# A two-block model on one core: in the second block, pairs of 64-row products alternate, low-rank columns are regrouped, inversion products are cut into 64-column halves, and the attention output is split late

## The chip, the core and the metric

The kernel runs on one core of one Trainium2 chip. The metric is the device time of one execution in microseconds (us), taken as the median of several runs.

## What is computed

Two layers are applied to a sequence of 1024 tokens of width 1024, all in float32. The change touches the mixer of the second layer alone. Cut to that part, the reference is:

```python
h = rms_norm(x, norm_mix_g)
u = h @ w_in                                  # 1024 x 4736
u_rwkv = centred_token_shift(u[:, :RWKV_COLS], mu_prev, mu_next)
q, k_att, v_att, gl_rwkv, gl_attn = split(u[:, RWKV_COLS:])
# rwkv7_bidir: r, k, v, g_lo and four low-rank inputs wf_lo, wb_lo, af_lo, ab_lo of 64 columns
decay  = exp(-DECAY_SCALE * sigmoid(w0 + tanh(w_lo) @ w_up))      # per direction
a      = sigmoid(a0 + a_lo @ a_up)                                # per direction
# per direction, 8 heads of 64, one step per token:
S = S * w_t - (S @ kk_t) (a_t * kk_t)^T + v_t k_t^T ;  y_t = S @ r_t
# banded_gqa_attention: 8 query heads, 2 key heads, window of 128 to both sides, blocks of 128
merged = sigmoid(gl_rwkv) * (y_rwkv @ w_proj_rwkv) + sigmoid(gl_attn) * (y_attn @ w_proj_attn)
x = x + merged @ w_out
```

The low-rank inputs lie in the columns of `w_in` in the order forward decay, backward decay, forward rate, backward rate, 64 columns each. After the mixer comes a mixture of 16 experts and a final norm.

## The kernel before

The function `phase_c` holds the mixer of the second layer. Features lie on the 128 partitions and tokens along the free dimension; one tile of 128 features holds two heads of 64. The recurrence over tokens is turned into chunks of 64 tokens.

`proj` multiplies the normed input with 37 tiles of 128 columns of `w_in`. Each of these jobs is two halves of 512 tokens, and each half is 24 products in a rounded float32 form (`mm3`, lines 332 to 334). `proj_split` prepares the weights of a job (ScalarE line 327, VectorE line 328). Tiles 13 and 14 are the low-rank inputs: 13 holds the decay columns of both directions, 14 the rate columns. Tiles 15 to 20 feed attention, 21 to 36 are gates. `choose` appends jobs to the list two ahead of the one that runs: the three tiles r, k, v of the next pair of heads once the pair before has its low-rank outputs, and else the next of the others.

`prep(p)` runs four times in a row, once for each pair of heads p, and waits first for its tiles r, k, v. It transposes v (line 1474), sums squares over each head with the product against `hones` (line 1482: a 128-column stationary operand and a moving operand of two columns), and makes the low-rank outputs (line 1508, four products of 64 rows and 512 tokens for each direction d: both halves of the decay, then both of the rate). VectorE then forms the operands AR and BK (lines 1517 to 1543). The products of line 1561 follow in bursts of four, one burst for each head h, each with 64 rows, 128 stationary and 128 moving columns. VectorE masks the result out of PSUM (lines 1564 and 1565), and after two bursts four transposes follow (line 1569, out of PSUM by ScalarE line 1570). There are 64 such bursts. At the end of a prep comes another product against `hones` (line 1610).

`invert(p)` inverts a 32 by 32 triangular matrix per chunk in 31 steps on VectorE (lines 1632, 1633) and completes it with two groups of 16 products (lines 1655, 1673: 128 rows, 128 stationary columns of which each half serves one direction, 32 moving columns). `chain` steps through the 16 chunks in both directions; each step loads its operands by DMA and multiplies in bursts whose 64-column halves alternate. `attn_scores` makes one product of 64 rows for each of 8 heads and 8 blocks (line 1723, up to 384 moving columns), each put out by VectorE (line 1725). `attn_values` multiplies with the values; for each block it then scales (line 1796) and splits the result into a rounded part and a remainder (ScalarE line 1804, GpSimd line 1805). `post_rwkv`, `merge_rwkv` and `merge_attn` finish the mixer.

The order of the instructions on each engine is fixed at build time. All these functions are generators; `weave` resumes the first one in the list whose condition holds in the times that a planner (`Model`) has worked out. A `yield` of a number asks to be resumed so many nanoseconds later, `K.room(tag)` when a PSUM bank is free by the plan, `K.when(...)` when operands are there. In the list, `inverts` and `preps` stand ahead of `chain`, and `proj` stands behind these, so the projection fills what the others leave. PSUM has four banks under the tag `mm` and four under `sm`. SBUF blocks of one size come from a ring.

```python
def room(self, tag):
    return lambda: self.clock.room(tag)
```

## Time and profile before

| | |
|---|---|
| median of 3 runs | 3086.57 us (3083.51 to 3089.09) |
| time of the profiled execution | 3083.45 us |
| its span | 3081.7 us |
| TensorE busy | 2856.3 us (93%) |
| VectorE busy | 2122.4 us (69%) |
| ScalarE busy | 1357.7 us (44%) |
| GpSimd busy | 434.1 us (14%) |
| mean granted TensorE clock | 0.953 |

The span is the time from the first to the last instruction of the profiled execution. In the views of the trace, PE is TensorE's matmul, PEld its weight load, DVE VectorE, ACT ScalarE, POOL GpSimd and SP SyncE, which issues most DMAs. A float32 product appears as two PE records; a product in the rounded form as one. A record's duration is a latency: consecutive records overlap, so a group's cost is read from start to start, or from the group's busy time, which counts overlaps once. PEclk is the share of the full TensorE clock that was granted: 1.00 is 2.4 GHz and 0.50 is 1.2 GHz.

### The profile page before, as it was taken

How to read it: one execution, taken by the hardware profiler on the slowest of the kernel's cores; microseconds unless marked ns; L12 is line 12 of the kernel's file. 1: busy time of each engine (PE TensorE's matmuls, PEld its weight loads, DVE VectorE, ACT ScalarE, POOL GpSimd, SP SyncE). 2: the span in 40 equal slices, each digit the busy share in tenths (PEclk: the TensorE clock that was granted, in tenths of full speed). 3: DMA queues.
4: the chain of work that ended last, by engine and by line, in shares of the span. 5: the costliest groups of instructions: out<-in, count | busy, mean ns of one | idle time of the engine just before them, and what ended most of it. 6: DMA issues, size and time to landing. Idle time of an engine off the chain costs nothing. (4 is left out here: it accounts for less than half of the span.)

```text
span 3081.7 us, 41330 instructions
## 1 busy us (share of the span) xinstructions
PE 2856.3 (93%) x15743; PEld 2300.4 (75%) x15743; DVE 2122.4 (69%) x3039; ACT 1357.7 (44%) x2152; POOL 434.1 (14%) x506
## 2 busy tenths in 40 slices
PE   7989989999999999889999998998799769999995
PEld 3878778788888888677777776776477658888884
DVE  5574655666656666745768675678755989999995
ACT  5442344432122222343343442454522258888885
POOL 2410001000000000322111011034101301211112
PEclk8989999999999999999989988999899989999998
DMA  7421122311111111414444545385143679999994
GB/s 276 151 69 42 55 72 86 116 48 41 42 62 48 48 48 39 127 55 121 112 110 117 123 109 134 110 262 155 52 146 125 247 282 384 395 392 396 396 377 135
DMA packets 381693, 470.42 MB, mean 153 GB/s; under 512 B 151184, under 2 KB 282679, under 8 KB 381495
## 3 DMA queue, kind: packets, MB, share of 16 engines
q1 hardware_dynamic: 374519, 450.97, 43.8%
q0 software_dynamic: 6976, 16.81, 2.3%
q8 instruction: 124, 2.03, 0.3%
q14 instruction: 74, 0.61, 0.1%
HBM read 390.12 MB, written 77.59 MB: 152 GB/s over the span
## 5 line engine op out<-in xcount | busy, mean ns | idle before, releaser
L328 DVE TENSOR_TENSOR wl<-wr,wh 128x1024 fp32r<-128x1024 f32 x534 | 639.7, 1229 | 234.4 <-ACT wh L327 214.8
L327 ACT ACTIVATE wh<-wr 128x1024 fp32r<-128x1024 f32 x536 | 554.1, 1061 | 94.5 <-PE mm L334 52.9
L332 PE MATMUL mm<-h,wh 128*128 128x512 f32 x1296 | 525.6, 406 | 0.0
L334 PE MATMUL mm<-h,wl 128*128 128x512 f32 x1296 | 512.1, 395 | 12.7 <-DVE wl L328 12.7
L333 PE MATMUL mm<-h,wh 128*128 128x512 f32 x1296 | 511.9, 395 | 0.0
L334 PEld LDWEIGHTS mm<-h,wl 128*128 128x128 f32 x1296 | 247.6, 191 | 67.1 <-DVE wl L328 14.0
L332 PEld LDWEIGHTS mm<-h,wh 128*128 128x128 f32 x1296 | 247.9, 191 | 63.2 <-issue 8.3
L333 PEld LDWEIGHTS mm<-h,wh 128*128 128x128 f32 x1296 | 248.1, 191 | 47.5 <-DVE h L535 0.2
L1176 DVE SCALAR_TENSOR_TENSOR u<-pad,par,u 128x1024 f32<-128x1024 f32 x176 | 225.7, 1282 | 6.8 <-ACT u L1173 3.4
L332 PE MATMUL mm<-wh,eh 128*128 128x512 f32 x512 | 201.1, 393 | 0.0
L333 PE MATMUL mm<-wl,eh 128*128 128x512 f32 x512 | 199.7, 390 | 0.0
L334 PE MATMUL mm<-wh,el 128*128 128x512 f32 x512 | 199.6, 390 | 0.0
L1250 DVE TENSOR_TENSOR yacc<-yacc,mm 128x512 f32<-128x512 f32 x144 | 98.9, 686 | 74.8 <-PE mm L334 74.0
L333 PE MATMUL mm<-wl,ah 128*128 128x512 f32 x352 | 137.7, 391 | 1.1 <-DVE wl L328 1.1
L332 PE MATMUL mm<-wh,ah 128*128 128x512 f32 x352 | 138.1, 392 | 0.6 <-ACT wh L327 0.6
L334 PE MATMUL mm<-wh,al 128*128 128x512 f32 x352 | 137.4, 390 | 0.0
L2405 POOL DMA_INDIRECT xacc<-ys,slot x32 | 72.1, 2253 | 440.5 <-ACT ys L2404 435.9
L1162 ACT ACTIVATE pad<-mm 128x512 f32<-128x512 f32 x44 | 26.4, 601 | 238.3 <-PE mm L334 238.3
L332 PE MATMUL mm<-hh,wh 128*128 128x512 f32 (+1 forms) x296 | 119.5, 404 | 0.0
L333 PE MATMUL mm<-hh,wh 128*128 128x512 f32 (+1 forms) x296 | 115.6, 391 | 0.8 <-DVE hh L716 0.8
L334 PE MATMUL mm<-hh,wl 128*128 128x512 f32 (+1 forms) x296 | 115.1, 389 | 0.0
L334 PEld LDWEIGHTS mm<-wh,el 128*128 128x128 f32 x512 | 96.4, 188 | 20.4 <-DVE el L2361 0.2
(468 smaller groups left out, 5693.5 us busy)
## 6 DMA issues: line engine op xcount, KB each, us to landing
wr<-in_exp_w_gate_dram SPq DMA_DIRECT2D x128, 512.0 KB
wr<-in_exp_w_up_dram SPq DMA_DIRECT2D x128, 512.0 KB
wr<-in_exp_w_down_dram SPq DMA_DIRECT2D x128, 512.0 KB
wr<-in_w_in_dram SPq DMA_DIRECT2D x62, 512.0 KB
wr<-in_w_ada_dram SPq DMA_DIRECT2D x48, 512.0 KB
wr<-in_w_up_dram SPq DMA_DIRECT2D x44, 512.0 KB
KB<-KB SPq DMA_DIRECT2D x32, 512.0 KB
wr<-in_w_down_dram SPq DMA_DIRECT2D x22, 512.0 KB
```

What stands on the lines that cost most here:

```text
L327: self.nc.scalar.activation(hi, src, AF.Copy)
L328: (eng or self.nc.vector).tensor_tensor(lo, src, hi.bitcast(F32), SUB)
L332: t.matmul(ps, wh, xh, start=start, stop=False)
L333: t.matmul(ps, wh, xl, start=False, stop=False)
L334: t.matmul(ps, wl, xh, start=False, stop=stop)
L1162: nc.scalar.activation(p[:, 1 + 8 * m:9 + 8 * m, 1:65], ps.rearrange("p (r c) -> p r c", c=64), AF.Copy)
L1176: nc.vector.scalar_tensor_tensor(u, p[:, i // 3:i // 3 + 16, i % 3:i % 3 + 64], w(i), u, op0=MUL, op1=ADD)
L1250: nc.vector.tensor_add(yacc[t][:, s], yacc[t][:, s], ps)
L2405: nc.gpsimd.indirect_dma_start(out=xacc[c], out_offset=bass.IndirectOffsetOnAxis(ap=slot[:, e - 1:e], axis=0), in_=ys[:, s], in_offset=Non ...
```

## The change

The diff below is cut to its core. Six things change, all in the mixer of the second layer.

The products of line 1561 of the two heads, which use rows 0 to 63 and 64 to 127, are issued alternately into two PSUM banks, in 32 bursts of eight in place of 64 bursts of four. The wait between them goes from 900 ns after each to 1800 ns after both.

The low-rank columns are loaded so that tile 13 holds decay and rate of the forward direction and tile 14 those of the backward one. Decay and rate of one direction then use different rows and alternate in pieces of 256 tokens. For this, each of the two weight loads becomes two DMAs, the per-column shift factors are loaded once more in the new order (four small DMAs), and the tanh runs on half the partitions of each of the two tiles.

The scores of two heads alternate in pieces of 128 keys. The products against `hones` and the two products of the inversion are each cut into two halves of 64 stationary columns. The conditions `K.room(tag, 2)` ask for two free banks.

The attention result is kept in float32 blocks, and a new generator `split_att` splits it in two parts on ScalarE and VectorE once the chain is done. The planner's cost for 64-row products is changed to match.

```diff
-            if f(ins[1]) <= 64:
+            if f(ins[1]) <= 64 or ins[0].ap[0][1] == 64:
                 return max(f(ins[0]), f(ins[1])) / 1.2 + 8
-    def room(self, tag):
-        return lambda: self.clock.room(tag)
+    def room(self, tag, n=1):
+        return lambda: max(self.clock.room(tag, 4 - i) for i in range(n))
...
+        for n in ("mu_prev", "mu_next"):
+            lo = a[n + "_2"][0][13 * 128:15 * 128].rearrange("(i d j) -> i d j", i=2, j=64)
+            items.append((n + "_l", [(lo[0], slice(0, 64)), (lo[1], slice(64, 128))], 2))
...
-    job = lambda i: (w_in, 0, 128 * i, 128, 8)
+    job = lambda i: (w_in, 0, (64 * i + 832, 64 * i + 960) if i in (13, 14) else 128 * i, 128, 8)
...
-            if i == 13:
-                nc.scalar.activation(u, u, AF.Tanh)
+            if i in (13, 14):
+                nc.scalar.activation(u[0:64], u[0:64], AF.Tanh)
...
-            nc.tensor.matmul(ps[:, t, :], sq[:, 128 * t:128 * t + 128], hones, start=True, stop=True)
+            for q in hq:
+                nc.tensor.matmul(ps[q, t, :], sq[:, 128 * t + q.start:128 * t + q.stop], hones, start=True, stop=True)
...
-            for i in range(2):
-                for m in range(2):
-                    ps = K.sm()
-                    q = slice(64 * d, 64 * d + 64)
-                    nc.tensor.matmul(ps, Z["up"][q, i, 128 * p:128 * p + 128], R[13 + i][q, off[m]:off[m] + 512], start=True, stop=True)
+            for m in range(2):
+                yield K.room("sm", 2)
+                ps = [K.sm() for _ in range(2)]
+                for n in range(0, 512, 256):
+                    for i in range(2):
+                        q = slice(64 * i, 64 * i + 64)
+                        nc.tensor.matmul(ps[i][:, n:n + 256], Z["up"][q, d, 128 * p:128 * p + 128],
+                                         R[13 + d][q, off[m] + n:off[m] + n + 256], start=True, stop=True)
...
-                    for h in range(2):
-                        q = slice(64 * h, 64 * h + 64)
-                        yield K.room("sm")
-                        ps = K.sm([128, 4, 128])
-                        for i in range(4):
-                            c = 4 * b + i
-                            nc.tensor.matmul(ps[:, i, :], BK[g][q, c].rearrange("p s t -> p (s t)"),
-                                             AR[g][q, c].rearrange("p s t -> p (s t)"), start=True, stop=True)
+                    yield K.room("sm", 2)
+                    pss = [K.sm([128, 4, 128]) for h in range(2)]
+                    for i in range(4):
+                        c = 4 * b + i
+                        for h in range(2):
+                            q = slice(64 * h, 64 * h + 64)
+                            nc.tensor.matmul(pss[h][:, i, :], BK[g][q, c].rearrange("p s t -> p (s t)"),
+                                             AR[g][q, c].rearrange("p s t -> p (s t)"), start=True, stop=True)
...
-                        yield 900
+                    yield 1800
...
-            nc.tensor.matmul(ps[:, c, :], OF[c // 8][:, c % 8, :], Dt[:, c, :], start=True, stop=True)
+            for q in hq:
+                nc.tensor.matmul(ps[q, c, :], OF[c // 8][:, c % 8, q], Dt[:, c, :], start=True, stop=True)
...
-                yield K.room("mm")
-                q = slice(64 * (h % 2), 64 * (h % 2) + 64)
-                ps = K.mm()
-                nc.tensor.matmul(ps[:, :n], q_fm[15 + h // 2][q, 128 * b:128 * b + 128], kd[h // 4][q, 128 * lo:128 * hi], start=True, stop=True)
+                if h % 2 == 0:
+                    yield K.room("mm", 2)
+                    pss = [K.mm() for _ in range(2)]
+                    for i in range(lo, hi):
+                        for x, q in enumerate(hq):
+                            nc.tensor.matmul(pss[x][:, 128 * (i - lo):128 * (i - lo) + 128], q_fm[15 + h // 2][q, 128 * b:128 * b + 128],
+                                             kd[h // 4][q, 128 * i:128 * i + 128], start=True, stop=True)
...
-                nc.scalar.activation(hi_, y[:, 2 * kp:2 * kp + 2, :], AF.Copy)
-                nc.gpsimd.tensor_tensor(lo_, y[:, 2 * kp:2 * kp + 2, :], hi_.bitcast(F32), SUB)
+                nc.vector.tensor_tensor(YQ[b // 4][kp][:, :, tok:tok + 128], po[:, kk, :], y[:, kk, :], MUL)
...
+    def split_att():
+        yield K.after("chain")
+        for m in range(2):
+            yield K.after(("yq", 4 * m + 3))
+            YA[m] = hl_blocks(K, "ya", 2)
+            for kp in range(2):
+                K.split(YQ[m][kp], YA[m][0][kp], YA[m][1][kp])
+                yield False
```

## Rows read from the trace of the kernel before

**Rows 1.** Busy time by stretch: length, PE PEld DVE ACT POOL, PEclk, DMA, GB/s.
```profile
1386.00:1888.00 502.00, 497.07 (x2387) 384.56 (x2385) 342.36 (x592) 198.62 (x289) 66.59 (x58) 0.93 0.46 114
1888.00:1980.00 92.00, 76.02 (x368) 62.67 (x367) 48.85 (x101) 26.74 (x37) 10.02 (x12) 0.87 0.32 87
1980.00:2145.00 165.00, 140.74 (x2744) 113.44 (x2744) 122.59 (x258) 83.71 (x217) 54.86 (x74) 0.95 0.82 238
2145.00:2220.00 75.00, 54.54 (x250) 32.97 (x249) 56.34 (x108) 35.99 (x90) 21.53 (x22) 0.80 0.08 25
1563.55:1587.44 23.89, 23.89 (x72) 17.03 (x72) 9.40 (x14) 14.74 (x23) 0.84 (x1) 0.50 0.55 123
```

**Rows 2.** End of prep 0, start of prep 1, timeline: start us, length.
```profile
1483.84 2.25 PE L1610 MATMUL sm<-hones,ks 128*128 128x2 f32 x15
...
1506.54 1.03 PE L1474 MATMUL sm<-ident,u 128*128 128x128 f32 x8
```

**Rows 3.** After prep 3, timeline of DVE: first inversion step, its wait.
```profile
1914.22 0.20 DVE L1632 TENSOR_TENSOR tmp<-N,M 128x31 f32<-128x31 f32 x1 [23.28 <-POOL M L1627]
```

**Rows 4.** Groups of PE by line: busy us, mean ns, idle before.
```profile
L1561 PE MATMUL sm<-AR,BK 64*128 64x128 f32 x512 | 73.9, 285 | 0.8 <-DVE BK L1543 0.8
L1508 PE MATMUL sm<-u,lora 64*128 64x512 f32 x64 | 40.2, 772 | 0.0
L1673 PE MATMUL sm<-Dt,HT 128*128 128x32 f32 x128 | 24.0, 362 | 0.8 <-ACT HT L1646 0.8
L1655 PE MATMUL sm<-Dt,OF 128*128 128x32 f32 x128 | 17.0, 295 | 0.7 <-ACT Dt L1646 0.7
L1610 PE MATMUL sm<-hones,ks 128*128 128x2 f32 x64 | 8.3, 260 | 3.3 <-DVE ks L1607 3.3
L1482 PE MATMUL sm<-hones,sq 128*128 128x2 f32 x64 | 7.4, 246 | 0.0
L1723 PE MATMUL mm<-katt,qatt 64*128 64x384 f32 (+1 forms) x128 | 36.5, 534 | 0.1
```

**Rows 5.** One burst of line 1561 between projection records, timeline of PE.
```profile
1414.45 0.39 PE L334 MATMUL mm<-h,wl 128*128 128x512 f32 x1
1414.77 1.16 PE L1561 MATMUL sm<-AR,BK 64*128 64x128 f32 x8
1415.85 0.50 PE L332 MATMUL mm<-h,wh 128*128 128x512 f32 x1
```

**Rows 6.** Block 1, alternating 64-row products at PEclk 0.50, timeline of PE.
```profile
169.73 3.79 PE L962 MATMUL sm<-v,kt 64*128 64x128 f32 x32
173.45 0.79 PE L332 MATMUL mm<-hh,wh 128*128 128x512 f32 x1
...
196.17 0.42 PE L979 MATMUL sm<-kq,kq 64*128 64x128 f32 x1
196.18 0.42 PE L980 MATMUL sm<-kq,kq 64*128 64x128 f32 x1
```

**Rows 7.** Chain bursts of alternating 64-column halves, timeline of PE (PEclk 1.00).
```profile
1988.53 1.15 PE L1953 MATMUL sm<-XS,LA 128*64 128x64 f32 x32
1989.51 0.29 PE L1920 MATMUL mm<-LR,XS 128*64 128x64 f32 x4
```

**Rows 8.** Low-rank and inversion products at full, then half clock, timeline of PE.
```profile
1519.99 3.70 PE L1508 MATMUL sm<-u,lora 64*128 64x512 f32 x8
...
1568.49 3.78 PE L1508 MATMUL sm<-u,lora 64*128 64x512 f32 x4
1572.20 7.03 PE L1673 MATMUL sm<-Dt,HT 128*128 128x32 f32 x32
```

**Rows 9.** Waits, 1386 to 1888 us: who, releaser, us, times, longest.
```profile
DVE TA L1564 <- PE sm L1561: 53.2, 32, 3.1
```

**Rows 10.** Attention's split in the kernel before, and VectorE's split of 1024 columns.
```profile
L1805 POOL TENSOR_TENSOR ya<-rd,ya 128x256 fp32r<-128x256 f32 x16 | 11.4, 730 | 62.3 <-ACT ya L1804 62.3
L328 DVE TENSOR_TENSOR wl<-wr,wh 128x1024 fp32r<-128x1024 f32 x31 | 37.8, 1221 | 9.0 <-ACT wh L327 8.8
```

More of the change, by code (lines that the diff above doesn't have):

```diff
@@ L344, in wraw @@
         t = self.blk([128, kt, nc_], name="wr")
+        if isinstance(c0, tuple):
+            n = nc_ // len(c0)
+            for i, c in enumerate(c0):
+                self.nc.sync.dma_start(t[:, :, n * i:n * i + n], w[r0:r0 + kt * 128, c:c + n].rearrange("(k p) c -> p k c", p=128))
+            return t
         self.nc.sync.dma_start(t, w[r0:r0 + kt * 128, c0:c0 + nc_].rearrange("(k p) c -> p k c", p=128))
@@ L1313, in phase_c @@
     nc.vector.tensor_scalar(ka[:, 4:8], ka[:, 0:4], -1.0, 1.0, op0=MUL, op1=ADD)
+    hq = [slice(64 * h, 64 * h + 64) for h in range(2)]
     hones = K.own("hones", [128, 2])
@@ L1503, in prep @@
             th = [K.blk([128, T], name="th") for _ in range(2)]
[L1504 to L1508 removed]
+            for m in range(2):
[6 more added lines that the diff above has]
+                                         R[13 + d][q, off[m] + n:off[m] + n + 256], start=True, stop=True)
+                for i in range(2):
                     dst = rv(th[i])[:, off[m]:off[m] + 512]
[L1510 to L1511 removed]
+                    nc.scalar.activation(dst, ps[i], AF.Tanh, bias=hb[:, 8 * i + 4 * d + p:8 * i + 4 * d + p + 1], scale=0.5)
+                yield True
             tw, ta = th
@@ L1609, in prep @@
         for t in range(8):
-            nc.tensor.matmul(ps[:, t, :], ks[:, 128 * t:128 * t + 128], hones, start=True, stop=True)
+            for q in hq:
+                nc.tensor.matmul(ps[q, t, :], ks[:, 128 * t + q.start:128 * t + q.stop], hones, start=True, stop=True)
         nc.vector.tensor_copy(bonus[:, :, 2 * p:2 * p + 2], ps)
@@ L1654, in invert @@
         for c in range(16):
-            nc.tensor.matmul(ps[:, c, :], OF[c // 8][:, c % 8, :], Dt[:, c, :], start=True, stop=True)
+            for q in hq:
+                nc.tensor.matmul(ps[q, c, :], OF[c // 8][:, c % 8, q], Dt[:, c, :], start=True, stop=True)
         K.mark(("off", p))
@@ L1672, in invert @@
         for c in range(16):
-            nc.tensor.matmul(ps[:, c, :], HT[c // 8][:, c % 8, :], Mt[:, c, :], start=True, stop=True)
+            for q in hq:
+                nc.tensor.matmul(ps[q, c, :], HT[c // 8][:, c % 8, q], Mt[:, c, :], start=True, stop=True)
         yield K.when(ps)
@@ L1703, in phase_c @@
     YA = {}
-    P, ST, Yo, VA = {}, {}, {}, {}
+    P, ST, YQ = {}, {}, {}
     def attn_scores():
@@ L1795, in attn_values @@
             yield K.when(po)
-            nc.vector.tensor_tensor(y, po, y, MUL)
-            ST.pop(b)
-            yield False
             tok = b % 4 * 128
             if tok == 0:
-                YA[b // 4] = hl_blocks(K, "ya", 2)
+                YQ[b // 4] = [K.blk([128, 2, 512], name="yq") for _ in range(2)]
             for kp in range(2):
-                hi_, lo_ = (YA[b // 4][i][kp][:, :, tok:tok + 128] for i in range(2))
-                nc.scalar.activation(hi_, y[:, 2 * kp:2 * kp + 2, :], AF.Copy)
-                nc.gpsimd.tensor_tensor(lo_, y[:, 2 * kp:2 * kp + 2, :], hi_.bitcast(F32), SUB)
-            K.mark(("ya", b))
+                kk = slice(2 * kp, 2 * kp + 2)
+                nc.vector.tensor_tensor(YQ[b // 4][kp][:, :, tok:tok + 128], po[:, kk, :], y[:, kk, :], MUL)
+            ST.pop(b)
+            K.mark(("yq", b))
             yield True
@@ L1809, in attn_values @@
         kd.clear()
+    def split_att():
[6 more added lines that the diff above has]
+                yield False
+            YQ[m].clear()
+            K.mark(("ya", m))
     MG, GT = {}, {}
@@ L1848, in merge_attn @@
         yield K.after("merge_rwkv")
-        yield K.after(("ya", 3))
+        yield K.after(("ya", 0))
         W = [K.wsplit(K.wraw(w_proj[1], 0, 4, 256 * i, 256)) for i in range(4)]
@@ L1856, in merge_attn @@
             if i == 0:
-                yield K.after(("ya", 4 * m + 3))
+                yield K.after(("ya", m))
             if n < 7:
@@ L2110, in phase_c @@
     st.load(2)
-    return MG, x2d, (proj_first(), proj_split(), *before, inverts(), preps(), chain(), values_bonus(), proj(), post_rwkv((3, 2, 1, 0)), attn_values(), post_rwkv((4, 5, 6, 7)), split_y(), attn_scores(), merge_attn(), merge_rwkv())
+    return MG, x2d, (proj_first(), proj_split(), *before, inverts(), preps(), chain(), values_bonus(), proj(), post_rwkv((3, 2, 1, 0)), attn_values(), post_rwkv((4, 5, 6, 7)), split_y(), attn_scores(), split_att(), merge_attn(), merge_rwkv())
 def phase_d(K, MG, x2d, before):
```

19 lines of the change are left out of this document (10 added, 9 removed).

## The prediction, made before the changed kernel was run

> **What bounds the kernel now.** I read first the busy time by stretch over the second mixer, with the borders set at the start of the first prep, the end of the last, the first step of the chain that has all its operands, and the chain's end [rows 1]. Between 1386 and 1888 us PE is busy for 497.1 of 502 us and VectorE for 342.4: the four preps and the projection that fills around them are bound by PE's work. From 1888 to 1980 us PE is busy for 76.0 of 92 us. There the last inversion sets the end: its first step on VectorE waited 23.3 us for a GpSimd memset [rows 3], which stands in GpSimd's queue behind copies that wait for a load. From 1980 to 2145 us the chain goes on at a DMA share of 0.82 with PE at 140.7 of 165 us; it is not bound by PE alone. From 2145 to 2220 us PE is idle a quarter of the time and VectorE is busy for 56.3 of 75 us.
>
> The second look is at whether work saved in a prep can shorten the first stretch. Prep 0 starts its last products at 1483.8 us and prep 1 begins at 1506.5 us [rows 2]: it waits for its own tiles of the projection. In that hole PE runs projection, so a prep that ends earlier finds a longer hole only if PE has no less to do. As PE is never idle, each microsecond of PE work taken out of a prep moves everything behind it, the hole included. That holds as long as projection jobs are left to fill with; PE's 76.0 us after the last prep are mostly such jobs, so the supply doesn't run out before.
>
> The third look is at what the lines of the change cost on PE [rows 4], and the fourth at records that already alternate elsewhere in this kernel [rows 6, 7].
>
> **Products of line 1561.** A burst of four products is eight records. From the projection record before it to the one behind it are 1.40 us [rows 5]; less the 0.21 us that 512 columns take at 2.4 GHz, a burst costs 1.19 us. 64 bursts are 76 us, and the group's busy time says 73.9 [rows 4]. What two heads side by side cost is shown by block 1: two products of 64 rows on the two halves of the rows start 10 ns apart [rows 6]. There 32 records, 16 pairs, fill 3.72 us at half clock, so 0.116 us a pair at full clock, and eight pairs 0.93 us. That is a burst of today without its edges, for two heads. I take half of 73.9: **37 us**. The bounds are 27 (half of the 53.2 us for which VectorE is seen to wait for this line [rows 9]) and 42 (64 bursts of 1.19 become 32 of 1.05).
>
> **Low-rank products.** They are busy for 40.2 us [rows 4] in eight passes. A pass at full clock takes 3.70 us, and half a pass at half clock 3.78 [rows 8]. The changed pass has eight pairs of 256 columns, which is half the time at either clock: 20 us. If the slow passes stay as slow and the edges eat part, 8 x 1.7 = 14; if all run at full clock, 40.2 - 8 x 1.85 = 25. I take **17 us**, nearer to the lower one, since edges stay.
>
> **Products against hones.** 8.3 + 7.4 us in eight groups [rows 4], 1.96 each. The new form has 32 records, 16 pairs of 64-column halves. No row has such halves with two moving columns; the nearest is the chain, where 16 pairs with 64 moving columns take 0.98 us from the start of one burst to the next line [rows 7]. That is 0.98 us less a group, and at most 8 us. The other end is nothing gained. I take **5 us**, near to the chain's row, less two changes of the array's layout.
>
> **Products of the inversion.** 24.0 + 17.0 us in eight groups [rows 4], one of them 7.03 us at half clock [rows 8]. The new form has 64 records, 32 pairs, 1.96 us by the chain's row at full clock. At the clocks of today half is saved, 20; at full clock 41.0 - 8 x 1.96 = 25; if the halves don't overlap well, 10. I take **18 us**; the last two groups lie on the path to the chain itself.
>
> The Trainium skill speaks against these last two: TensorEngine Tiling (Array Packing), Performance Considerations, says that a product with one moving column takes as long as one with 60, and that no tiling should be taken from a dimension that is already small. With 2 and 32 moving columns this is the case here. No row here decides it, since the chain's halves move 64 columns.
>
> **Sum of the first stretch.** 37 + 17 + 5 + 18 = 77 us. All of it is PE work in a stretch that PE bounds.
>
> **Scores of attention.** 36.5 us [rows 4]. The new form has 24 pairs of heads with three blocks of keys and eight with two, that is 88 block pairs or 176 pairs of records; at 0.116 us, 20.4 us, so 16 us of PE are saved. They lie where PE is not the bound [rows 1]. I take a third, **5 us**; the ends are -3 (each pair now waits for two free banks of `mm`, behind which the chain's outputs queue too) and 16.
>
> **The late split.** It takes 11.4 us off GpSimd and adds four VectorE operations of 1.22 us [rows 10], 4.9 us, half of them right behind the chain, where VectorE is the busiest engine. For GpSimd the waits for ScalarE before these operations go too, 62.3 us in all [rows 10], in which the small operations of `post_rwkv` stood in the same queue. I set it at nothing; -5 and +5 are the ends.
>
> **The rest.** The extra weight DMAs of tiles 13 and 14 are issued on SP while block 1 still runs on PE, and the four small DMAs at the kernel's start join 18 such loads in the code; the second tanh is on ScalarE, 198.6 of 502 us busy [rows 1]. Cover is PE's work in each case; without it they would cost some 3 us. The wait of 1800 ns after both heads is the two of 900 ns put together; queued behind it are only the four transposes, and the projection runs meanwhile. VectorE's four masks of a pair come later than two of them do now, but no engine waits for them before the pair's blocks are written.
>
> **Total.** 77 + 5 = 82 us. Against the profiled execution 3083.45 - 82 = 3001.5; the median of the runs is 3.1 us above that execution, so the forecast is **3004 us**.
>
> **Rivals.**
> *The clock gives more.* PEclk is 0.93 in the first stretch [rows 1], which is half clock for some 70 us, or 35 us lost; it falls around the inversion and the low-rank products, as in the 23.89 us at 0.50 [rows 1, 8]. If short, full products keep it up, some 25 us come on top of the halves counted: 2979 us.
> *VectorE takes over.* It has 342 us to do in what would become 430 us, in one queue with the 62 steps of an inversion. VectorE waits for line 1561 for 53.2 us in all [rows 9]; if only half of that turns into time, 26.6, the other terms at half, 20, and the scores give nothing: 3040 us. Against it: VectorE still has 20% to spare.
> *Small halves don't pay.* By a fixed cost for each record, the halves of hones and inversion would be twice as many records of today's length: 15.7 and 41.0 us more rather than 23 less. 37 + 17 + 5 - 56.7 = 2 us saved: 3084 us, no change. The rule of the Trainium skill named above would bring this.
> *The pairs don't overlap.* Then only the column halves gain, 23 us: 3064 us. Rows 6 speak against it.
> *Slower: two free banks are late.* Each pair of line 1561 and each half of a low-rank pass asks for two of the four `sm` banks, 48 times, and these are freed by VectorE, which may be in an inversion or a weight split of 1.22 us [rows 10]. What the prep then waits is filled with projection, which is gone by the end of prep 3. The gain is used up at 82/48 = 1.7 us a wait. At 2.0 us the kernel takes 3100 us. Four masks and a split make 2.9 us, of which 1.8 is covered, so 1.1 is the likelier ceiling.
>
> **How the numbers follow.** The forecast (2987 to 3022) has 0.50, the clock 0.15, VectorE 0.19, small halves 0.04, no overlap 0.04, late banks 0.08. Faster by over 0.2% (6 us, about what a measurement of this kernel can tell from no change) is 0.50 + 0.15 + 0.19 + 0.04 = 0.88, same 0.04, slower 0.08. The range from 2970 to 3052 takes in the forecast with the bounds of its terms, VectorE, and most of the clock's case, some 0.8.
>
> **What will show it.** Right: line 1561 in 32 bursts of 16 records of about 1.2 us and a group of about 37 us; records of the two heads 10 ns apart; a group of about 20 us for the low-rank products, 20 for the scores; the last prep ending near 1815 us with PE as full as before; a chain of about 165 us. Wrong: PE idle between 1386 us and the end of the last prep, with VectorE or a bank named as the releaser; groups of hones or inversion as long as before; the stretch behind the chain longer by what the first one lost.

## The result, and the profile after

The changed kernel takes 3016.30 us (median of 4 runs, 3015.44 to 3022.27) where the kernel before took 3085.04 us beside it (median of 4, 3081.05 to 3089.09). The ratio is 0.9781, with a 95% interval from 0.9763 to 0.98: 68.7 us faster, where the forecast said 82. Its profiled execution took 3017.06 us, with a span of 3015.3 and a mean granted clock of 0.956.

The size was nearly right and the way to it was not. Busy time by stretch of the changed kernel (length, PE, PEld, DVE, ACT, POOL, PEclk, DMA share, GB/s), with borders as in [rows 1]: start of the first prep, end of the last prep, first step of the chain with all its operands, end of the chain, router (the first step of the mixture of experts, which follows the mixer).

```profile
100.00:1364.00 1264.00, 1222.39 (x6029) 1016.35 (x6028) 792.22 (x936) 413.81 (x729) 104.20 (x146) 0.99 0.21 67
1364.00:1842.00 478.00, 438.79 (x2858) 349.69 (x2857) 344.58 (x595) 202.32 (x294) 67.78 (x60) 0.95 0.48 121
1842.00:1951.00 109.00, 88.20 (x617) 67.65 (x616) 75.14 (x174) 47.45 (x105) 7.88 (x10) 0.83 0.29 80
1951.00:2121.00 170.00, 148.32 (x2990) 127.75 (x2988) 132.26 (x293) 94.30 (x243) 53.20 (x70) 0.97 0.78 225
2121.00:2270.00 149.00, 116.84 (x476) 92.19 (x475) 97.06 (x128) 38.41 (x53) 19.71 (x15) 0.87 0.36 118
```

The same view of the kernel before, the two stretches that [rows 1] don't have:

```profile
100.00:1386.00 1286.00, 1229.37 (x6032) 1022.10 (x6031) 791.34 (x936) 414.23 (x729) 104.17 (x146) 0.98 0.21 66
2145.00:2339.00 194.00, 167.59 (x770) 123.35 (x769) 131.04 (x226) 74.63 (x163) 24.40 (x26) 0.91 0.29 91
```

Stretch by stretch: block 1 is 22 us shorter, the preps 24 (502 to 478), the last inversion 17 longer (92 to 109), the chain 5 longer (165 to 170), and what follows the chain 45 shorter (194 to 149). Together block 2 gives 47 us, block 1 gives 22, and 3 are lost behind the router: 66 us between the two spans.

The stretch of the last inversion hides two changes. In the kernel before it holds the 23.28 us for which VectorE waits for GpSimd's memset [rows 3]. In the changed kernel the same step starts right behind the last prep without that wait; instead, VectorE's queue holds attention's operations by now, and they wait for the scores (a row of DVE's timeline, then one of its waits from 1842 to 1960 us):

```profile
1844.08 0.21 DVE L1654 TENSOR_TENSOR tmp<-N,M 128x31 f32<-128x31 f32 x1
```

```profile
DVE p L1753 <- PE mm L1749: 18.2, 4, 14.4
```

From the end of the last prep to the router it is 451 us before and 429 after:

```profile
1888.30:2339.20 450.90, 384.25 (x3877) 299.20 (x3878) 302.48 (x584) 184.78 (x417) 89.28 (x112) 0.92 0.49 144
1840.90:2269.80 428.90, 354.26 (x4082) 288.34 (x4082) 304.64 (x594) 181.24 (x402) 80.79 (x94) 0.90 0.51 151
```

TensorE's work did what was forecast. Add up PE over the four stretches of block 2: 497.07 + 76.02 + 140.74 + 167.59 = 881 us before, and 438.79 + 88.20 + 148.32 + 116.84 = 792 after, 89 less. But block 2 is only 47 us shorter. The other 42 us turned into idle time of TensorE, 34 of them in the preps, where it had been idle for 5 us and now is for 39. What it waits for there (waits of PE from 1380 to 1870 us; line waited at, releaser, us in total, times, longest):

```profile
PE sm L1581 <- DVE BK L1563: 17.1, 6, 5.8
PE sm L1632 <- DVE ks L1628: 7.3, 4, 4.4
PE sm L1678 <- ACT Dt L1668: 3.7, 2, 2.6
PE sm L1581 <- DVE TR L1586: 3.7, 2, 2.5
```

The groups of the changed lines (line 1581 was 1561, 1526 was 1508, 1697 and 1678 were 1673 and 1655, 1632 and 1498 were 1610 and 1482, 1749 was 1723), to be read against [rows 4]:

```profile
L1581 PE MATMUL sm<-AR,BK 64*128 64x128 f32 x512 | 44.0, 305 | 20.8 <-DVE BK L1563 17.1 <-DVE TR L1586 3.7
L1526 PE MATMUL sm<-u,lora 64*128 64x256 f32 x128 | 19.8, 418 | 0.3 <-ACT th L1530 0.3
L1697 PE MATMUL sm<-Dt,HT 128*64 128x32 f32 x256 | 9.4, 224 | 3.9 <-ACT HT L1668 3.9
L1678 PE MATMUL sm<-Dt,OF 128*64 128x32 f32 x256 | 8.3, 223 | 3.8 <-ACT Dt L1668 3.7
L1632 PE MATMUL sm<-hones,ks 128*64 128x2 f32 x128 | 5.2, 210 | 7.3 <-DVE ks L1628 7.3
L1498 PE MATMUL sm<-hones,sq 128*64 128x2 f32 x128 | 4.4, 199 | 0.0
L1749 PE MATMUL mm<-katt,qatt 64*128 64x128 f32 x352 | 28.5, 294 | 2.5 <-DVE p L1753 2.5
```

The preps' own lines are 80 us shorter. 28 more triples of projection, a triple being the three products of the rounded form, are done among them (450 records of each of the three products instead of 422, 0.227 us from one product to the next, 19 us), and PE is busy for 58 us less in 24 us less time.

What the preps wait for shows in the timeline, at the place where a prep goes from its first direction to its second. In pair 1 and pair 3 of the changed kernel (start us, length, line; the last burst of the first direction, the first product of the inversion of the pair before, the second direction's low-rank products):

```profile
1521.48 1.16 PE L1581 MATMUL sm<-AR,BK 64*128 64x128 f32 x16
...
1529.89 2.06 PE L1678 MATMUL sm<-Dt,OF 128*64 128x32 f32 x64 [1.11 <-ACT Dt L1668]
1531.87 1.13 PE L1526 MATMUL sm<-u,lora 64*128 64x256 f32 x8
...
1762.96 1.21 PE L1581 MATMUL sm<-AR,BK 64*128 64x128 f32 x16
...
1785.12 2.08 PE L1678 MATMUL sm<-Dt,OF 128*64 128x32 f32 x64 [2.57 <-ACT Dt L1668]
1787.13 2.08 PE L1526 MATMUL sm<-u,lora 64*128 64x256 f32 x8
```

The second direction starts right behind the inversion's product of line 1678, each time, and 9, 14 and 23 us after the first direction has ended. The code has the reason: a prep waits at the end of its first direction for the mark `off` of the pair before (line 1611; 1590 before), since the block OF exists once. No row of the waits names this, as TensorE runs projection meanwhile. It closes a loop: a prep's end frees the inversion of its pair (62 steps on VectorE), that reaches `off`, this releases the next pair's second direction, and its end frees the next inversion. In the kernel before, the place looks like this (the low-rank products follow at 1568.49 [rows 8]):

```profile
1560.24 1.16 PE L1561 MATMUL sm<-AR,BK 64*128 64x128 f32 x8
1561.33 5.04 PE L1655 MATMUL sm<-Dt,OF 128*128 128x32 f32 x32
```

From the ends and starts of these groups in each trace, for pairs 1, 2 and 3, in us:

| kernel | from a prep's end to `off` | second direction starts behind `off` by | period of the preps | all preps |
|---|---|---|---|---|
| before | 80.3, 75.1, 75.6 | 2.1, 1.1, 2.1 | 138.1, 131.6, 132.5 | 501.7 |
| changed | 69.9, 70.0, 75.1 | 0, 0, 0 | 124.0, 126.0, 128.8 | 476.5 |
| no price (experiment 2) | 68.2, 67.3, 65.8 | 7.7, 11.0, 11.2 | 124.1, 121.2, 120.1 | 453.3 |
| price in block 1 (5) | 67.7, 65.7, 51.6 | 10.0, 11.7, 36.8 | 126.6, 126.4, 132.5 | 473.1 |
| less VectorE (7) | 29.2, 36.7, 36.7 | 43.9, 41.5, 39.9 | 113.3, 118.5, 118.3 | 447.8 |
| less projection (8) | 80.5, 81.2, 66.7 | 0, 0, 0 | 139.1, 138.9, 110.2 | 484.6 |
| late `off` (9) | 104.8, 81.2, 77.2 | before it | 114.7, 125.3, 121.2 | 451.9 |
| late `off`, old price (11) | 64.3, 65.5, 66.7 | 11.3, 11.3, 17.3 | 117.3, 120.3, 123.3 | 445.7 |

### The profile page after: what moved, and what is told of

Same layout as the page of the kernel before. It is cut to its first block, busy times and chain, and to the rows that moved or that the text cites. A ratio compares the mean times of both kernels' runs of the same rounds, so it can differ in the third digit from the quotient of the medians.

```text
span 3015.3 us, 42642 instructions
## 1 busy us (share of the span) xinstructions
PE 2759.8 (92%) x16415; PEld 2248.3 (75%) x16415; DVE 2127.9 (71%) x3052; ACT 1356.8 (45%) x2141; POOL 425.5 (14%) x490
## 5 line engine op out<-in xcount | busy, mean ns | idle before, releaser
L333 PE MATMUL mm<-wh,ah 128*128 128x512 f32 x352 | 138.1, 392 | 0.6 <-ACT wh L328 0.6
```

Of the source, the lines that this page charges most:

```text
L333: t.matmul(ps, wh, xh, start=start, stop=False)
```

## The experiments

Times are compared by their ratio to the kernel before that ran beside them; the changed kernel's is 0.9781. The first four ask what each part brings alone.

**1. The planner's price, in block 1 alone.**

```diff
-            if f(ins[1]) <= 64:
+            if f(ins[1]) <= 64 or ins[0].ap[0][1] == 64 and self.pairs:
...
+            K.clock.pairs = True
...
+            K.clock.pairs = False
```

> The kernel before, with one thing of the change: the planner's new, lower price for 64-row products, and only around block 1's alternating products of two heads (lines 962 and 979/980 of before). The instructions are the same, only their order on the queues can differ. Theory A (the 22 us by which block 1 ends earlier in the changed kernel come from this price alone): the first preparation of block 2 starts near 1364 us instead of 1386.6, the rest moves along, and the time is 3063 us (3057 to 3070), a ratio near 0.993. Rival (block 1's gain comes from another part, say the regrouped weights or more buffers asked for at once): the start stays within 5 us of 1386.6 and the time within 6 us of before.

Measured: 3060.20 us, ratio 0.9929 (0.9914 to 0.9944), 22 us faster. The first prep starts at 1366.3 us. Theory A's start and time came out: an order that the planner writes differently, with the same instructions, shortens block 1. The waits of PE show where, in the kernel before and then in this one, up to 534 and 513 us (where the same work is done):

```profile
PE sm L992 <- DVE att L982: 16.0, 3, 6.3
```

```profile
PE sm L997 <- DVE att L987: 3.9, 2, 3.7
```

But the rest does not simply move along. The preps take 516 us instead of 502 and give 14 of block 1's 20 us back. What comes back behind them is the wait of [rows 3], which is gone here too: from the last prep's end to the router are 429.5 us instead of 450.9, with the instructions of the kernel before. The rows are the preps' busy time, VectorE's first step of the last inversion, and the busy time from there to the router.

```profile
1366.30:1882.00 515.70, 497.80 (x2385) 386.63 (x2384) 342.74 (x593) 198.26 (x289) 67.97 (x60) 0.93 0.45 111
1884.17 0.21 DVE L1637 TENSOR_TENSOR tmp<-N,M 128x31 f32<-128x31 f32 x1
1881.90:2311.40 429.50, 378.42 (x3875) 298.39 (x3875) 306.04 (x584) 184.21 (x416) 90.73 (x110) 0.92 0.50 151
```

**2. The changed kernel with the old price everywhere.**

```diff
-            if f(ins[1]) <= 64 or ins[0].ap[0][1] == 64:
+            if f(ins[1]) <= 64:
```

> The changed kernel, with the planner's old price for 64-row products everywhere, in block 1 and in block 2. Theory A (block 1's gain is the price): the first preparation starts near 1386 us again and 22 us are lost, so 3038 us (3028 to 3048), ratio 0.985, block 2 being moved alone. Rival one (the price also sets block 2's order: with the old one the planner believes a burst of line 1581 to last longer than it does and leaves TensorE empty): more is lost, 3050 us or above. Rival two (the old price makes the planner put the bursts later, where VectorE's operands are there, and so removes the 39 us for which TensorE waits in the preparations): less is lost, 3020 us or below.

Measured: 3019.51 us, ratio 0.9796 (0.9781 to 0.9811). Block 1 lost its gain (first prep at 1390.4 us), and yet the time is that of the changed kernel within the two intervals: rival two. The preps are 23 us shorter, and end at 1843.7 us where they end at 1840.9 in the changed kernel.

```profile
1390.40:1843.70 453.30, 418.26 (x2757) 335.24 (x2755) 340.31 (x592) 195.89 (x287) 64.44 (x58) 0.95 0.51 126
```

**3 and 4. The alternating products of two heads alone, and the 64-column halves alone, each on the kernel before.**

```diff
-                    for h in range(2):
-                        q = slice(64 * h, 64 * h + 64)
-                        yield K.room("sm")
-                        ps = K.sm([128, 4, 128])
-                        for i in range(4):
-                            c = 4 * b + i
+                    yield K.room("sm", 2)
+                    pss = [K.sm([128, 4, 128]) for h in range(2)]
+                    for i in range(4):
+                        c = 4 * b + i
+                        for h in range(2):
+                            q = slice(64 * h, 64 * h + 64)
```

> The kernel before, with the alternating products of two heads alone (line 1561 of before in bursts of 16 with two banks, and their new price around these bursts). In the changed kernel's trace this group is 30 us of TensorE shorter than in the trace of before. Theory P (as predicted: TensorE's work in the preparations sets the time): the whole 30 us come off, 3055 us (3050 to 3060). Theory V (behind the shorter bursts TensorE waits for VectorE's operands and masks, so that about a third of the saving shortens the preparations and some more comes back as projection done earlier): 3068 us (3060 to 3077), with TensorE idle in the preparations for 10 to 25 us instead of 5. Rival (two free banks come late): 3085 us or more.

```diff
-            nc.tensor.matmul(ps[:, t, :], sq[:, 128 * t:128 * t + 128], hones, start=True, stop=True)
+            for q in hq:
+                nc.tensor.matmul(ps[q, t, :], sq[:, 128 * t + q.start:128 * t + q.stop], hones, start=True, stop=True)
...
-            nc.tensor.matmul(ps[:, c, :], OF[c // 8][:, c % 8, :], Dt[:, c, :], start=True, stop=True)
+            for q in hq:
+                nc.tensor.matmul(ps[q, c, :], OF[c // 8][:, c % 8, q], Dt[:, c, :], start=True, stop=True)
```

> The kernel before, with the 64-column halves alone (the sums over a head's channels and the two products of the inversion, as halves that run side by side). In the changed kernel's trace these groups are 6 and 23 us of TensorE shorter. Theory P (TensorE's work sets the preparations): 3056 us (3050 to 3061). Theory V (VectorE's chain through the operands sets them by now): these products stand between VectorE's steps, and their saving shortens that chain only where it waits for them: 3070 us (3062 to 3078). Rival (small halves do not pay, since twice the instructions are issued): 3083 us or more.

Measured: 3056.41 us, ratio 0.9916 (0.9899 to 0.9932), 26 us; and 3051.43 us, ratio 0.9897 (0.988 to 0.9914), 32 us. Both times lie in theory P's ranges, but the preps do not bear it out. They are 21 and 18 us shorter than the 501.7 us of the kernel before, while TensorE is busy in them for 41 and 30 us less than its 496.8, and idle for 24 and 17 us where it was for 5. In experiment 3 that is theory V's sign. So either part alone turns some half of TensorE's saving there into shorter preps. The preps of the one and of the other:

```profile
1387.40:1867.90 480.50, 456.05 (x2367) 361.33 (x2366) 340.52 (x592) 197.95 (x288) 65.78 (x58) 0.92 0.48 119
```

```profile
1387.60:1871.20 483.60, 466.60 (x2705) 356.19 (x2703) 341.56 (x592) 197.52 (x287) 68.24 (x60) 0.96 0.47 118
```

The rest of the gain lies behind the preps: 444 us from the last prep's end to the router in experiment 3 and 433 in experiment 4, instead of 451. In experiment 3 the last inversion still waits for the memset of [rows 3], in experiment 4 it no longer does:

```profile
1892.71 0.20 DVE L1637 TENSOR_TENSOR tmp<-N,M 128x31 f32<-128x31 f32 x1 [22.15 <-POOL M L1632]
```

```profile
1874.32 0.21 DVE L1635 TENSOR_TENSOR tmp<-N,M 128x31 f32<-128x31 f32 x1
```

The three parts make 22 + 26 + 32 = 80 us alone, without the low-rank products, the scores and the late split, and 69 with all of them. Something stops the sum. It is not that TensorE is saved less: that is 89 us. One thing that can be counted only once is the wait for the memset: experiments 1 and 4 are both without it, and so is the changed kernel. Why GpSimd's memset comes earlier in them was not followed, and no run takes that wait out alone. The other is in the preps.

**5. The changed kernel with the new price in block 1 alone.** As in experiment 1, on the changed kernel.

> The changed kernel with the planner's new price only around block 1's alternating products, and the old one for every product of block 2. With the old price everywhere the preparations took 453 us (1390.4 to 1843.7) instead of 477 in the changed kernel, but block 1 lost its 22 us. Theory O (the new price shortens block 1 and lengthens the preparations, because the order written with it puts bursts on TensorE ahead of VectorE's operands): both gains add, the first preparation starts near 1366 us, the last ends near 1820, and the time is 2996 us (2988 to 3004), ratio 0.9715. Rival S (saturation: whatever starts earlier meets a later limit, such as the projection's weights or the chain's loads): the ratio stays within 0.002 of the changed kernel's 0.978, 3012 to 3022 us.

Measured: 3019.03 us, ratio 0.9805 (0.9791 to 0.9819). Theory O fell, and the time lies in rival S's range. Block 1 has its gain (first prep at 1367.1 us), and the preps give it back, as in experiment 1: they take 473 us with the same price in block 2 with which they took 453.

```profile
1367.10:1840.20 473.10, 421.41 (x2748) 337.49 (x2747) 341.48 (x593) 196.46 (x288) 67.09 (x60) 0.93 0.49 122
```

**6. The bursts of line 1581 planned 4 us later.**

```diff
-            yield False
+            end = K.clock.last + 4000
+            yield lambda: end
             K.mark(("ops", p, d))
```

> The changed kernel, with one step of its planned order moved: the bursts of line 1581 are asked for 4 us later than the planner's own time, so that projection is queued ahead of them. Theory O (TensorE's 39 us of idle time in the preparations come from bursts queued before VectorE's operands are there): TensorE's wait for BK in front of line 1581 (17.1 us) falls under 6 us, and the time falls by 8 to 18 us, 2998 to 3008. Theory V (VectorE's chain sets the preparations, and TensorE's idle time is only what is left): the wait falls too, but the preparations do not get shorter, and the time stays within 5 us of 3016 or rises.

Measured: 3027.49 us, ratio 0.9831 (0.9817 to 0.9846), 15 us slower than the changed kernel. The wait for BK goes and another, for the split weights of the projection, comes; the preps take 499.9 us. This is what theory V had, and theory O fell: taking this wait away doesn't shorten the preps. The edit also puts its 4 us into each direction of each prep, so it doesn't show that no other order would.

```profile
PE mm L335 <- DVE wl L329: 27.7, 5, 11.7
...
PE sm L1582 <- DVE BK L1563: 2.3, 2, 1.4
```

**7. Less VectorE.**

```diff
-        for s in range(31):
+        for s in range(31 if p == 3 else 15):
```

> The changed kernel, with 15 of the 31 steps of the inversion's recursion for the first three of the four pairs of heads (the rest of the inverse is left out): some 40 us less of VectorE within the preparations, nothing less on TensorE. Theory V (VectorE's busy time sets the preparations): the last preparation ends 25 us or more earlier than 1841 and the time is 2990 us or less. Theory O (the order on TensorE's queue and the delay of single operands set them, and not the sum of VectorE's work): the preparations end within 10 us of 1841, and the time is 3005 to 3020.

Measured: 2993.60 us, ratio 0.9727 (0.9705 to 0.9749). The last prep ends at 1814.3 us, 27 earlier, as theory V said; the time falls by 17 us by the ratios, between the two theories. The edit shortens the inversion (29 to 37 us to `off` instead of 70 to 75) and VectorE's sum (308.3 instead of 344.0 us) at once, so it doesn't tell which of them counts. Experiment 9 does.

**8. Less TensorE.**

```diff
-            K.mm3(ps[:, :n], wh[:, k, :], wl[:, k, :], x1, x2, k == 0, k == 7)
+            if less:
+                K.nc.tensor.matmul(ps[:, :n], wh[:, k, :], x1, start=(k == 0), stop=False)
+                K.nc.tensor.matmul(ps[:, :n], wl[:, k, :], x1, start=False, stop=(k == 7))
```

> The changed kernel, with two of the three products of each gate projection (the third is left out), which takes some 59 us of TensorE off the work that is queued between the preparations' bursts, and no VectorE work. Theory P (TensorE's work still sets block 2): the time falls by 45 us or more, 2971 or less, most of it from the preparations. Theory O/V (the preparations wait for operands and the projection only fills them): the preparations get shorter by less than 25 us with more idle time on TensorE, and the time falls by 15 to 40 us, as what is left over of the projection behind the chain disappears.

Measured: 3017.02 us, ratio 0.9797 (0.9777 to 0.9816): nothing. No theory had said nothing. The preps are longer by 8 us, with 67 us of TensorE idle; the clock is lower too (0.90 instead of 0.95), so of the 38 us of products that are missing in them (240 triples and 230 pairs where there were 450 triples) 20 show as less busy time, 437 to 417.

```profile
1365.80:1850.40 484.60, 417.34 (x2695) 333.59 (x2693) 342.61 (x594) 204.61 (x300) 67.16 (x60) 0.90 0.48 119
```

Here the loop lies open: each prep starts at the end of the one before, its first direction ends 33, 33 and 21 us before `off`, and the second one starts on the spot. The way from a prep's end to `off` has itself grown in two of the three pairs, to 80.5 and 81.2 us; why was not followed. This is pair 1:

```profile
1508.69 1.16 PE L1585 MATMUL sm<-AR,BK 64*128 64x128 f32 x16
...
1540.61 2.06 PE L1682 MATMUL sm<-Dt,OF 128*64 128x32 f32 x64 [0.80 <-ACT Dt L1672]
1542.60 1.13 PE L1530 MATMUL sm<-u,lora 64*128 64x256 f32 x8
```

**9. The wait for `off` moved behind the second direction.** The copies into OF go with it; the work is the same.

```diff
-                else:
-                    yield K.after(("off", p - 1))
...
+            if d == 1:
+                if p:
+                    yield K.after(("off", p - 1))
+                for e in range(2):
+                    for h in range(2):
+                        q = slice(64 * e + 32 * h, 64 * e + 32 * h + 32)
+                        for g in range(2):
+                            nc.scalar.activation(Z["OF"][g][q, :, q], TA[h][e][64 * h:64 * h + 32, 8 * g:8 * g + 8, 32:64], AF.Copy)
```

> The changed kernel, with one wait moved: in each preparation the wait for the first product of the inversion of the pair before (the mark off, which frees the block OF) stands at the end of the second direction instead of the end of the first, together with the copies into OF that need it. The work is the same. In the changed kernel's trace the second direction's low-rank products start at the very end of that product, 9, 14 and 23 us after the first direction's products have ended. Theory L (a loop of preparation, inversion, second direction, next inversion sets the period of 124 to 129 us, and neither the sum of TensorE's nor that of VectorE's work): these 46 us of waiting go, the stretch from the first preparation to the end of the last falls from 477 to 430 to 455 us and the time to 2985 us (2970 to 3000). Theory V (VectorE's sum of work): the waits are replaced by others, the stretch stays above 468 us, and the time is 3008 to 3025.

Measured: 2993.28 us, ratio 0.9701 (0.9688 to 0.9714): 25 us faster than the changed kernel by the ratios, for one wait at another place. Preps and time are inside theory L's ranges and outside theory V's, with VectorE's sum as before (341.0 us). Of the 25 us that the preps lose, 18 are in the three periods (9, 1 and 8). The other 7 are in the first prep, 90.7 us instead of 97.7, which waits for no `off`: the edit moves ScalarE's copies there too, and why that prep is shorter was not followed. In pair 1 the low-rank products now stand right behind the first direction, and 38 us before the inversion's product:

```profile
1516.05 1.16 PE L1581 MATMUL sm<-AR,BK 64*128 64x128 f32 x16
...
1520.54 2.00 PE L1526 MATMUL sm<-u,lora 64*128 64x256 f32 x16
...
1558.37 2.06 PE L1681 MATMUL sm<-Dt,OF 128*64 128x32 f32 x64
```

```profile
1365.00:1817.00 452.00, 419.44 (x2778) 335.91 (x2777) 341.02 (x593) 196.38 (x282) 67.25 (x60) 0.95 0.51 126
```

**10. In addition, the next pair's tiles chosen earlier.**

```diff
-        if pairs and (pairs[0] > 3 or ("th", pairs[0] - 1) in K.done):
+        if pairs and (pairs[0] > 3 or ("ks", pairs[0] - 1) in K.done):
```

> As the run before, and in addition the next pair's three projection tiles may be chosen as soon as the keys of this pair are scaled (the mark ks), instead of behind the first direction's low-rank products (the mark th), some 20 us earlier. Theory L: with the inversion's wait gone the next thing that a preparation waits for is its own three tiles, which now come earlier; another 5 to 20 us come off, 2975 us (2960 to 2990). Rival: the tiles were there in time, or the blocks that they take are missing elsewhere, and the time is that of the run before within 5 us, or more.

Measured: 2991.71 us, ratio 0.9695 (0.9682 to 0.9708). That is the rival: no change. The periods are those of experiment 9 to a tenth (114.7, 125.3, 121.2), and the preps start 16 to 22 us behind the one before as there. The mark isn't what holds the tiles back.

**11. Both moves, with the new price in block 1 alone.**

> Both moves of the run before (the wait for the inversion at the end of the second direction, the next pair's tiles chosen earlier) on the kernel that keeps the planner's old price in block 2 and has the new one in block 1 alone. There the preparations waited less for the inversion (the second direction started 10, 12 and 37 us behind it) and more for their tiles (23, 25 and 27 us behind the end of the preparation before). Theory L: the earlier tiles take 10 us or more off each of the three gaps, and the stretch falls from 473 to 430 to 450 us, the time to 2985 us (2970 to 3000). Rival (the price's gain in block 1 is lost behind the preparations whatever their length): 3012 us or more.

Measured: 2985.00 us, ratio 0.9675 (0.9662 to 0.9688). This is the fastest kernel of the study, 33 us below the changed one by the ratios. The preps take 446 us, in theory L's range, but not by the step that it named: the gaps in front of a prep are 21 to 25 us, only some 2 us shorter than in experiment 5. It is the second direction that is shorter, 42, 43 and 39 us from its low-rank products to its end instead of 49, 49 and 44.

```profile
1368.00:1813.70 445.70, 409.16 (x2751) 329.46 (x2749) 342.36 (x592) 195.19 (x284) 67.51 (x60) 0.97 0.52 128
```

**12. The kernel before with less TensorE.** As in experiment 8, for every second gate.

> The kernel before, with two of the three products for every second gate (eight of the fifteen gate projections of the stretch; the third product is left out), so 128 products of 0.227 us or 29 us less of TensorE in the preparations' stretch, and nothing else. Theory P (as predicted: in the kernel before TensorE's sum of work sets the preparations, 497 us busy of 502): the whole 29 us come off, 3057 us (3052 to 3063), the last preparation ending 25 to 30 us earlier than 1888. Theory L (there too the loop through preparation, inversion and second direction sets them, in whose trace the second direction's low-rank products start 2.1, 1.1 and 2.1 us behind the inversion's first product, and projection only fills): 10 us or less come off the stretch, TensorE is idle for 20 us or more in it, and the time is 3073 us or more.

Measured: 3100.55 us, ratio 1.0054 (1.0034 to 1.0073): slower. Theory P's numbers all fail; theory L's bounds hold (TensorE is idle for 33 us), but it named no reason for a loss. The preps hold 20 us less of products (313 triples and 119 pairs where there were 422 triples, 0.227 us each), they take 33 us more, and TensorE is no less busy in them, since its clock is lower (0.88 instead of 0.93). So the run doesn't tell whether TensorE's sum or the loop set the preps of the kernel before. What it does show is that this sum can't be worked out from the instructions alone.

```profile
1391.30:1925.90 534.60, 501.49 (x2297) 386.33 (x2296) 344.26 (x594) 198.84 (x291) 66.34 (x58) 0.88 0.43 108
```

## Why the prediction was right, and where it wasn't

**The lines on TensorE: right.** In the order of the prediction, forecast and measured [rows 4]: line 1561 37 and 73.9 - 44.0 = 29.9; low-rank products 17 and 40.2 - 19.8 = 20.4; hones 5 and 15.7 - 9.6 = 6.1; inversion 18 and 41.0 - 17.7 = 23.3. That is 77 and 79.7. The two heads overlap as [rows 6] promised: a burst of 16 records takes the 1.16 us that one of 8 took [rows 5]. The group of 44.0 is more than 32 such bursts, 37 us. Most of the other 7 us lie in bursts that come late: three that TensorE enters behind waits of 4.2 to 5.8 us for BK take 2.8 us each, with the granted clock at 0.50, and a fourth at that clock takes 2.08.

**Small halves.** The Trainium skill, TensorEngine Tiling (Array Packing), Performance Considerations, says that a product with one moving column takes as long as one with 60, and that no tiling factor should be taken from a dimension that is small already. The trace agrees with the first: in these halves a record takes 34 ns with 2 moving columns (1.10 us for 32 records), 32 ns with 32 (2.06 us for 64) and 31 with 64 (0.98 us for 32 [rows 7]). The second the prediction read against these halves, with a chance of 0.04, and that reading was wrong: the halves are cut from the 128 stationary columns, and the small dimension, the moving one, stays whole. The groups with 2 moving columns went from 15.7 to 9.6 us and those with 32 from 41.0 to 17.7, and the run with the halves alone is 32 us faster (experiment 4), 18 of them in the preps.

**The step that failed** is "as PE is never idle, each microsecond of PE work taken out of a prep moves everything behind it", and with it "all of it is PE work in a stretch that PE bounds". 77 us were booked there; the preps got 24 us shorter and TensorE idle for 34 more. An engine into whose gaps projection is woven can be 99% busy without setting the pace alone: in experiments 3 and 4 it has 41 and 30 us less to do in those same preps, which get 21 and 18 us shorter. The prediction's own sign for this came up: PE idle in the preps, with VectorE named as the releaser. Experiments 8 and 9 give the cause in the changed kernel: taking 38 us of TensorE's products away gives nothing, at a lower clock, and moving one wait of the loop gives 25 us, of which 18 are in the loop's periods. Experiment 7, which shortens a step of the loop, and VectorE's sum with it, takes 29 us off the periods (124.0, 126.0, 128.8 to 113.3, 118.5, 118.3) and nothing off the first prep. The change had shortened the loop only by what it took out of the loop's own steps: the three ways from a prep's end to `off` by 16 us in all, those from `off` to the next end (57.8, 56.5, 56.9 to 54.2, 56.0, 53.7) by 7.

**Why it came out near all the same.** This was luck: gains that stood nowhere in the sum made up for what it lost. One is the planner's price: the prediction costed the change of line 93 at nothing, though block 1's pairs of [rows 6] are 64-row products too. It shortens block 1 by 22 us (20 in experiment 1), but the preps then get longer, by 14 us in experiment 1 and by 20 in experiment 5 against 2, and on top of the other parts the price is worth next to nothing (experiments 2 and 5).

The other is behind the preps, 22 us from the end of the last one to the router. Two things differ there. The wait of 23 us for the memset, which the prediction had read as the end of the last inversion's stretch [rows 3], is gone. And TensorE does more projection among the preps, so that attention's scores start at 1859.9 us instead of 1975.4 and end at 2067.3 instead of 2235.9, ahead of the chain's end: the stretch behind the chain is 45 us shorter, and in the stretch of the last inversion, where VectorE is busy for 75.1 us instead of 48.9, attention's operations now stand between the inversion's. Which of the two brings the 22 us isn't shown. Experiment 1 speaks for the first: it is without the wait, its scores start 87 us behind the last prep as in the kernel before (19 in the changed kernel), and it has the same 429 us. Experiment 2 says that it isn't all: it has the wait again, 23.4 us long, and scores that start 82 us behind the last prep, and takes 436 us. No run held attention back.

**The smaller terms.** The scores save 36.5 - 28.5 = 8 us on TensorE, not 16; a half of what two overlapping heads should give is missing, and 5 us were booked. The late split has the four VectorE operations that the forecast named. Neither was tried alone, nor were the low-rank products.

**The rivals.** "VectorE takes over" named the right releaser and, for the changed kernel, the wrong reason: experiment 9 has the same VectorE sum and is 25 us faster. "Late banks" did not happen: waits for VectorE's masks are 3.7 us in all. "The clock gives more" gave little, 0.93 to 0.95 in the preps.

**Open.** Whether the loop or TensorE's sum set the preps of the kernel before: there the second direction starts 1 to 2 us behind `off`, with TensorE 99% busy, so both were close to it, and experiments 3 and 4 take out work that belongs to both. Also open is why the preps get longer when block 1 gets shorter (by 14 us in experiment 1, by 20 in experiment 5 against 2, at the same price), and what holds them in experiments 9 to 11, where TensorE is still idle for some 33 to 37 us.

## What to carry to other kernels

An engine that is filled from a list of other work can be busy while something else sets the pace; before you book its saving as time, look for the unit that repeats, take its period, and ask of each of its steps what it starts right behind of. A step that always starts within a tenth of a microsecond of one other event points to the loop, even when no row of the waits names it, and moving that wait can bring more than making its work cheaper. Gains of parts that were measured one at a time, 80 us here, don't add up when two of them come without the same wait, or once another loop is the longest; so look stretch by stretch where each gain lies before you put it down to the part that was tried.

## What the hardware did that was not expected

In the two runs with less projection (8 and 12) the mean granted clock in the preps was lower, 0.90 instead of 0.95 and 0.88 instead of 0.93, so that the work left took longer. Less work alone doesn't do that: the changed kernel has 58 us less in its preps than the kernel before, and the higher clock, 0.95 instead of 0.93. In experiment 12 TensorE waits for split weights for 19.2 us in its preps, in the kernel before for nothing. One of these waits is 5.17 us long; ahead of it the granted clock is 1.00, and the stretch behind it has the lower of the two levels, 0.50, which is 1.2 GHz (a row of PE's timeline, and busy time by stretch ahead of the wait and behind it):

```profile
1690.67 0.80 PE L334 MATMUL mm<-h,wl 128*128 128x512 f32 x1 [5.17 <-DVE wl L328]
```

```profile
1681.00:1685.00 4.00, 4.00 (x19) 3.30 (x19) 3.97 (x8) 0.60 (x1) 0.00 (x0) 1.00 0.41 89
1691.00:1701.00 10.00, 10.00 (x31) 7.27 (x31) 5.00 (x14) 1.65 (x2) 0.00 (x0) 0.50 0.55 168
```

Over the preps the lower clock made up for all of the 20 us of products that were missing there: TensorE was busy for 501.5 us against 496.8 with them.
